# Attention scores over 128 rows: the queries' low part padded with zeros

## The chip, the cores and the metric

The kernel runs on one core of one Trainium2 chip, in one launch. The metric is the device time of a run in microseconds (us). Of the kernel before there are three timed runs and one profiled execution.

## What is computed

The reference is a block of two layers over 256 tokens (`x`) and 256 context tokens (`ctx`), 1024 features wide, in float32. Layer 0 mixes by neighbourhood attention with 16 heads of 64 features, layer 1 by a gated linear recurrence; each is followed by a feed-forward part, and every step is modulated by vectors worked out from a condition. The change lies in the attention of layer 0:

```python
q, k, v = jnp.split(h @ w_qkv, 3, axis=-1)
q = rms_norm(q.reshape(B, n, NA_HEADS, NA_HEAD_DIM), q_gain) * scale
k = rms_norm(k.reshape(B, n, NA_HEADS, NA_HEAD_DIM), k_gain)
...
s_loc = jnp.einsum('bqhd,bjqwhd->bhqjw', q_row, k_win) + bias.transpose(0, 2, 1, 3)[None]
s_ctx = jnp.einsum('bqhd,bkhd->bhqk', q_row, k_c)
s = jnp.concatenate([s_loc.reshape(B, NA_HEADS, GRID_W, n_loc), s_ctx], axis=-1)
p = jax.nn.softmax(s.astype(jnp.float32), axis=-1).astype(v_win.dtype)
```

The grid has 4 rows of 64 columns. A latent token sees 16 columns of each of the 4 rows and the whole context; a context token sees the context.

## The kernel before

Products run in a rounded form of float32 (`F32R`). To keep the precision, each operand is split in a high part (the rounded value) and a low part (what is left), and a product is hi*hi + hi*lo + lo*hi. `prod` (L404 to L415) does this for all weights; its matmul is L410, the line that fills most of TensorE's time. `split` (L402, L403) makes the two parts of the weights, the high one on ScalarE, the low one on VectorE.

`setup` (L68 to L190) loads the inputs and does the first products of the attention's queries, keys and values while the modulation vectors are still being worked out (`ada_first`, L266). Its buffers lie in a pool that is closed at its end; the pool of the attention takes the same memory.

`na` (L451) goes over 4 groups of 4 heads. For each it makes queries, keys and values from weight blocks of 256 columns (L410, through `toks`), normalises queries and keys (L475 to L480), and calls `na_pair` for two pairs of heads. `ada` (L298 for the loads, L216 for the products) works out further modulation vectors on the side, from blocks `ada_raw` with two buffers. The output projection follows (L410 with `oh`, `ol`).

`na_pair` (L519) does one pair of heads:

- GpSimd builds the table `tb` of biases and masks: it clears a part (L523), loads four pieces through its own DMA queue (L531), changes the sign (L534) and masks (L537, L541). Two buffers take turns.
- TensorE transposes queries and keys (L550), so that a head's 64 features lie in 64 partitions, the first head's in the lower half, the second head's in the upper.
- Per head (`a` = 0, 1), a key tile `ks` holds the high part in the head's own half and the low part in the other half (L561, L562). A query tile `qs` holds the high part in both halves (L566). The queries' low part goes to the head's own half of one tile `ql` that both heads share (L567).
- `scores` (L574) makes the logits with two products: L577 over 128 rows gives q_hi * k_hi + q_hi * k_lo; L578 over the 64 rows of the head's own half adds q_lo * k_hi. Per pair, four calls have 512 columns of keys (two tiles of latent queries for each head), and four have 256 (the context's). That makes 64 of L577 and 64 of L578 in the kernel.
- The softmax: VectorE adds the bias and takes the minimum (L599, the signs being changed) or takes the minimum alone (L631), ScalarE takes the exponential (L582), VectorE scales (L583, L584), TensorE transposes (L611, L635), and the products with the values follow (L649, L657), then the split of the output (L663, L664).

The two heads of a pair run as two generators in turn. A scheduler of the framework orders the instructions of each engine before the run: it places products of the next group's weights (L410) between the steps of the softmax. Each engine works through its own list in order.

```python
nc.tensor.matmul(ps, qs[a][:, t], ks[a][:, kr], start=True, stop=False, skip_group_check=True)
nc.tensor.matmul(ps, ql[f, t], ks[a][f, kr], start=False, stop=True, skip_group_check=True)
```

Of the kernel before, what the change touches and what calls it, by code (L numbers as in the profile page):

```python
# [8 lines left out]
F32 = mybir.dt.float32  # L9
# [22 lines left out]
# which modulation vectors are worked out when  # L32
# [4 lines left out]
def cap(ap, off, dims):  # L37
    """A free pattern of one's own over the partitions of ap."""
    return bass.AP(ap.tensor, ap.offset + off, [list(ap.ap[0])] + [list(d) for d in dims])


class Block:
# [19 lines left out]
    def mixed(self):  # L62
        """Banks of the three tags in turn, where nothing else asks for them."""
        self.turn = (getattr(self, "turn", -1) + 1) % 7
        return self.bank(("mm", "ax0", "ax1", "mm", "ax0", "ax1", "mm")[self.turn])

# [1 line left out]
    def setup(self):  # L68
# [16 lines left out]
        with ExitStack() as ctx:  # L85
# [56 lines left out]
            for k in range(KT):  # L142
                if k == 4:
                    # the factors of the first norm, in all partitions
# [13 lines left out]
            # the first products start on the features whose modulation is there already; one accumulation  # L158
            # group per bank
# [48 lines left out]
    def ada_rows(self, tiles, cs=None):  # L208
        """The products of silu(c), silu(c_ctx) with 4 blocks of 256 columns, as columns over the features."""
# [21 lines left out]
    def ada_put(self, l, m, k0, nj, cols, j0):  # L231
        """cols: the features of nj blocks from block j0 on, to be those from k0 on of vector m."""
# [20 lines left out]
    def ada_first(self, ip, qd):  # L253
        """Shift and scale of layer 0's first norm, for a quarter of the features."""
# [36 lines left out]
    def ada(self, l, params, pool=None):  # L291
        """Modulation vectors of layer l, as columns over the features, for both streams."""
        nc = self.nc
        for m in params:
            def tiles():
                for k in range(KT):
                    w = (pool or self.apool).tile([P, D], F32, name="ada_raw", tag="ada_raw")
                    nc.sync.dma_start(w, self.in_ada_w[l, k * P : (k + 1) * P, m * D : (m + 1) * D])  # L298
                    yield w

            self.ada_put(l, m, 0, 4, self.ada_rows(tiles()), 0)

    def ada_aside(self, params, pool, eng=None):
        """The same, step by step: the sums over blocks of 128 by the vector engine, those within by TensorE."""
        nc = self.nc
        eng = eng or nc.vector
        for l, m in params:
            # what follows layer 1's mixing is asked for the latents alone
# [20 lines left out]
    def norm_add(self, k, r):  # L329
        nc = self.nc  # L330
        if k == 0:
            nc.scalar.square(self.acc[:, r], self.x[k][:, r])
            if r.start == 0:
                # has the table of the function in place by the time that norm_end asks for it
# [37 lines left out]
    def weights_in_ctx(self, ap):  # L372
        """The same, in the context's half of h, which nothing else needs any more."""
# [10 lines left out]
    def weights(self, ap, pieces=4, pool=None):  # L384
        """A block of weights [nk*128, 256] as its two parts."""
# [19 lines left out]
    def prod(self, out, pairs, start=True, stop=True):  # L405
        """out += sum over the pairs of (hi, lo) of both sides."""
# [12 lines left out]
    def feat(self, out, w, m, r):  # L419
        """out [128 features of the block's half m, tokens r]"""  # L420
# [4 lines left out]
    def toks(self, out, w, tt, ks=range(KT), start=True, stop=True):  # L425
        """out [128 tokens of tile tt, the block's 256 features]"""
# [4 lines left out]
    def rsqrt(self, u):  # L431
        """u ** -0.5 of a few columns."""
# [18 lines left out]
    def na(self):  # L451
# [4 lines left out]
        ol = [np_.tile([P, T], F32R, name=f"ol{k}", bufs=1) for k in range(KT)]  # L456
        wq = self.in_na_w_qkv[0]
# [61 lines left out]
    def na_pair(self, np_, pr, j, qn, v, oh, ol):  # L519
# [5 lines left out]
        for u in range(2):  # L525
            # partition 64 u + i: row 1 - u of the tile's two, column 63 - i; with the sign changed, as the
            # logits' (their minimum is then the bias that the exponential asks for)
# [17 lines left out]
        # per head: queries [hi; hi] and keys [hi; lo], one above the other (its own half first), and  # L545
        # the queries' low parts; the queries of each tile go from the last to the first
# [7 lines left out]
        ql = np_.tile([P, T], F32R, name="ql", tag="ql", bufs=1)  # L554
        qs, ks = [], []
        for a in range(2):
# [8 lines left out]
            for half in (own, other):  # L565
                nc.scalar.activation(cap(qa[half], P - 1, back), src, AF.Copy, scale=self.q_gain[own])  # L566
            nc.vector.scalar_tensor_tensor(  # L567
                cap(ql[own], P - 1, back), src, self.q_gain[own], cap(qa.bitcast(F32)[own], P - 1, back),
# [5 lines left out]
        def scores(ps, a, q, kr):  # L574
            f = slice(64 * a, 64 * a + 64)
            t = slice(q * P, (q + 1) * P)
            nc.tensor.matmul(ps, qs[a][:, t], ks[a][:, kr], start=True, stop=False, skip_group_check=True)  # L577
            nc.tensor.matmul(ps, ql[f, t], ks[a][f, kr], start=False, stop=True, skip_group_check=True)  # L578
# [166 lines left out]
    def hgrn(self):  # L745
# [66 lines left out]
        for mc in range(4):  # L812
# [13 lines left out]
            if mc < 3:  # L826
                # one accumulation group for the bank: the heads come one after the other
# [14 lines left out]
    def hgrn_head(self, gp, h, m, sg, v, q):  # L842
        nc = self.nc
        # slots of xq: q forward, k forward, k backward, q backward
# [14 lines left out]
        # states after the context, one per direction  # L859
# [31 lines left out]
        # the products q k, by levels of blocks of 1, 2, 4, ... tokens: those within 32 tokens  # L891
        # lie in dc, the others in am
# [27 lines left out]
        for lg in range(7):  # L920
# [30 lines left out]
            for dr in range(2):  # L951
                # forward: q of odd blocks and k of even ones; backward: k of odd and q of even
# [16 lines left out]
        # through the whole of what comes before: the states' share  # L969
# [16 lines left out]
        else:  # L986
            # no other table is asked for until the norm that follows
# [11 lines left out]
    def finish(self, ctx):  # L999
# [4 lines left out]
        def after(mt, s, c):  # L1004
# [7 lines left out]
            # the last ones go out each on its own  # L1012
# [66 lines left out]
```

## Time and profile before

| | |
|---|---|
| time, three runs | 1185.1, 1185.15, 1188.06 us (median 1185.15) |
| profiled execution: its span | 1180.4 us; its own time is not listed apart, and the fastest run lies 4.7 us above it |
| busy share of the span | PE 98%, PEld 84%, DVE 67%, ACT 43%, POOL 6% |
| mean granted TensorE clock | 0.997 |
| HBM read | 166.82 MB, 142 GB/s over the span |

The profile names the engines PE (TensorE's products), PEld (its weight loads), DVE (VectorE), ACT (ScalarE), POOL (GpSimd) and SP (SyncE, here a DMA queue). The span is the time from the first to the last instruction of one execution. Products are pipelined on PE: a row's duration overlaps the next row's, and its end is modelled, so the distance between the starts of two rows tells how fast they follow each other.

### The profile page before, as it was taken

How to read it: one execution, taken by the hardware profiler on the slowest of the kernel's cores; microseconds unless marked ns; L12 is line 12 of the kernel's file. 1: busy time of each engine (PE TensorE's matmuls, PEld its weight loads, DVE VectorE, ACT ScalarE, POOL GpSimd, SP SyncE). 2: the span in 40 equal slices, each digit the busy share in tenths (PEclk: the TensorE clock that was granted, in tenths of full speed). 3: DMA queues.
4: the chain of work that ended last, by engine and by line, in shares of the span. 5: the costliest groups of instructions: out<-in, count | busy, mean ns of one | idle time of the engine just before them, and what ended most of it. 6: DMA issues, size and time to landing. Idle time of an engine off the chain costs nothing.

```text
span 1180.4 us, 21338 instructions
## 1 busy us (share of the span) xinstructions
PE 1155.7 (98%) x8539; PEld 989.7 (84%) x8539; DVE 786.3 (67%) x1872; ACT 502.1 (43%) x1079; POOL 76.5 (6%) x119
## 2 busy tenths in 40 slices
PE   6989999999999999999999999999999999999998
PEld 5967779786798788778888789979797989999998
DVE  4588676866679583845373668686868687665543
ACT  5346553736544322221332344434344355555442
POOL 1224232320000000000000000000000000000000
PEclk9989999999999999999999999999999999999999
DMA  9863372235116462646372552212232336655662
GB/s 330 267 184 88 86 167 73 51 85 179 56 52 217 142 228 74 194 146 221 105 234 91 173 176 71 96 63 95 72 108 73 108 113 237 219 177 185 201 211 89
DMA packets 134402, 169.23 MB, mean 143 GB/s; under 512 B 4608, under 2 KB 122272, under 8 KB 134304
## 3 DMA queue, kind: packets, MB, share of 16 engines
q1 hardware_dynamic: 132368, 164.64, 42.1%
q0 software_dynamic: 1728, 3.17, 3.1%
q8 instruction: 67, 1.10, 0.4%
q14 instruction: 31, 0.25, 0.1%
q10 hardware_dynamic: 208, 0.07, 0.0%
HBM read 166.82 MB, written 1.05 MB: 142 GB/s over the span
## 4 chain that ended last, share of the span: by engine, by line
PE 91%; DVE 5%; DMA 3%; ACT 1%; issue 0%; ACTq 0%; SPq 0%
PE mm L410 50%; PE ax L410 27%; PE ax L578 2%; PE ada_ps L216 2%; PE ax L577 2%; DMA ada_raw<-in_ada_w_dram 1%; PE ax L611 1%; PE ax L649 1%; DVE w_lo L403 1%; PE ax L900 1%; PE ax L883 1%; PE ada_ps L266 1%; DMA xt<-in_ctx_dram 1%; PE ax L946 1%; PE ax L635 1%; PE ax L550 0%
## 5 line engine op out<-in xcount | busy, mean ns | idle before, releaser
L403 DVE TENSOR_TENSOR w_lo<-w_raw,w_hi 128x512 fp32r<-128x512 f32 (+1 forms) x448 | 273.7, 647 | 129.1 <-ACT w_hi L402 126.7
L402 ACT CAST w_hi<-w_raw 128x512 fp32r<-128x512 f32 (+1 forms) x448 | 237.8, 583 | 229.4 <-PE mm L410 100.4
L410 PE MATMUL mm<-hl,w_hi 128*128 128x256 f32 (+1 forms) x608 | 201.3, 332 | 0.0
L410 PE MATMUL mm<-hh,w_lo 128*128 128x256 f32 (+1 forms) x608 | 200.6, 330 | 0.0
L410 PE MATMUL mm<-hh,w_hi 128*128 128x256 f32 (+1 forms) x608 | 198.4, 328 | 0.0
L410 PE MATMUL ax<-hh,w_lo 128*128 128x256 f32 (+1 forms) x400 | 131.1, 328 | 0.2 <-DVE w_lo L403 0.2
L410 PE MATMUL ax<-hh,w_hi 128*128 128x256 f32 (+1 forms) x400 | 131.0, 328 | 0.0
L410 PE MATMUL ax<-hl,w_hi 128*128 128x256 f32 (+1 forms) x400 | 130.9, 327 | 0.0
L410 PE MATMUL mm<-w_hi,hh 128*128 128x256 f32 x448 | 128.0, 286 | 0.8 <-ACT hh L366 0.8
L410 PE MATMUL mm<-w_hi,hl 128*128 128x256 f32 x448 | 127.4, 284 | 0.0
L410 PE MATMUL mm<-w_lo,hh 128*128 128x256 f32 x448 | 127.2, 284 | 0.0
L410 PEld LDWEIGHTS mm<-hl,w_hi 128*128 128x128 f32 x608 | 114.1, 188 | 11.3
L410 PEld LDWEIGHTS mm<-hh,w_lo 128*128 128x128 f32 x608 | 114.1, 188 | 10.9
L410 PEld LDWEIGHTS mm<-hh,w_hi 128*128 128x128 f32 x608 | 113.8, 188 | 11.2 <-ACT hh L366 0.8
L319 DVE SCALAR_TENSOR_TENSOR ada_acc<-ada_raw,cs,ada_acc 128x1024 f32<-128x1024 f32 x63 | 79.0, 1280 | 18.7 <-DMA ada_raw<-in_ada_w_dram 18.5
L410 PEld LDWEIGHTS mm<-w_hi,hh 128*128 128x128 f32 x448 | 85.6, 191 | 6.4 <-issue 4.7
L410 PEld LDWEIGHTS mm<-w_hi,hl 128*128 128x128 f32 x448 | 85.1, 190 | 3.6 <-issue 3.1
L410 PEld LDWEIGHTS mm<-w_lo,hh 128*128 128x128 f32 x448 | 85.0, 190 | 2.9 <-issue 2.7
L410 PEld LDWEIGHTS ax<-hh,w_hi 128*128 128x128 f32 x400 | 75.1, 188 | 7.9 <-ACT w_hi L402 0.8
L410 PEld LDWEIGHTS ax<-hh,w_lo 128*128 128x128 f32 x400 | 75.0, 188 | 7.5 <-DVE w_lo L403 0.4
L410 PEld LDWEIGHTS ax<-hl,w_hi 128*128 128x128 f32 x400 | 75.1, 188 | 7.3
L694 ACT CAST mid_h<-sa 128x512 fp32r<-128x512 f32 (+1 forms) x44 | 22.5, 512 | 91.8 <-DVE sa L691 91.8
(277 smaller groups left out, 2150.4 us busy)
## 6 DMA issues: line engine op xcount, KB each, us to landing
w_raw<-in_ffn_w_in_dram SPq DMA_DIRECT2D x44, 1024.0 KB, 5.0
ada_raw<-in_ada_w_dram SPq DMA_DIRECT2D x80, 512.0 KB, 4.5
w_raw<-in_hg_w_in_dram SPq DMA_DIRECT2D x20, 1024.0 KB, 4.8
w_raw<-in_na_w_qkv_dram SPq DMA_DIRECT2D x9, 1024.0 KB, 5.0
ada_first<-in_ada_w_dram SPq DMA_DIRECT2D x32, 256.0 KB, 5.8
w_raw<-in_ffn_w_out_dram SPq DMA_DIRECT2D x8, 896.0 KB, 4.6
w_raw<-in_ffn_w_out_dram SPq DMA_DIRECT2D x8, 768.0 KB, 4.3
w_raw<-in_ffn_w_out_dram SPq DMA_DIRECT2D x8, 640.0 KB, 4.2
```

The source lines that it names most:

```text
L216: nc.tensor.matmul(ps[32 * j : 32 * j + 32, 0:256], cs[:, k, :], w[:, j * 256 : (j + 1) * 256], start=(k == 0), stop=(k == last), tile_pos ...
L266: nc.tensor.matmul(ps[32 * j : 32 * j + 32, 0:P], self.cs[:, k, :], w[:, j // 2, (j % 2) * P : (j % 2 + 1) * P], start=(k == 0), stop=(k = ...
L319: eng.scalar_tensor_tensor(acc[s], w, c, acc[s], op0=ALU.mult, op1=ALU.add)
L402: self.nc.scalar.copy(wh[:, ks], raw[:, ks])
L403: self.nc.vector.tensor_tensor(wl[:, ks], raw[:, ks], wh.bitcast(F32)[:, ks], op=ALU.subtract)
L410: self.nc.tensor.matmul(out, a, b, start=(start and i == 0 and j == 0), stop=(stop and i == n - 1 and j == 2), skip_group_check=True,)
L577: nc.tensor.matmul(ps, qs[a][:, t], ks[a][:, kr], start=True, stop=False, skip_group_check=True)
L578: nc.tensor.matmul(ps, ql[f, t], ks[a][f, kr], start=False, stop=True, skip_group_check=True)
L611: nc.tensor.transpose(tp[:, kt * P : (kt + 1) * P], sb[:, kt * P : (kt + 1) * P], self.ident)
L635: nc.tensor.transpose(tp[:, kt * 256 + i * P : kt * 256 + (i + 1) * P], sb[:, i, kt * P : (kt + 1) * P], self.ident)
L649: nc.tensor.matmul(o[64 * a : 64 * a + 64, 0:256], v[:, kt, j * P + 64 * a : j * P + 64 * a + 64], pts[a][0][:, kt], start=(kt == 0), stop ...
L694: nc.scalar.copy(mh, sa)
```

## The change

The tile `ql` becomes two tiles, one per head, made once at the start of the attention. GpSimd writes zeros into the other head's half of each. The low part is written to the head's own half as before. The second score product takes all 128 rows of the query tile and of the key tile; the rows with zeros add nothing to the sum. `ql0` takes the slot in which the norm's sum `acc` is kept later, `ql1` lies in the attention's pool. The changed file has also lost its comments and gained two lines, so that lines of `na_pair` carry other numbers (L577 and L578 are L579 and L580, L523 and L531 are L527 and L535).

```diff
     def na(self):
...
         ol = [np_.tile([P, T], F32R, name=f"ol{k}", bufs=1) for k in range(KT)]
+
+        self.ql = [self.spool.tile([P, T], F32R, name="ql0", tag="acc", bufs=1), np_.tile([P, T], F32R, name="ql1", bufs=1)]
+        for a in range(2):
+            nc.gpsimd.memset(self.ql[a][64 - 64 * a : 128 - 64 * a].bitcast(F32), 0.0)
         wq = self.in_na_w_qkv[0]
...
         back = [[P, 4], [-1, P]]
-        ql = np_.tile([P, T], F32R, name="ql", tag="ql", bufs=1)
         qs, ks = [], []
...
             nc.vector.scalar_tensor_tensor(
-                cap(ql[own], P - 1, back), src, self.q_gain[own], cap(qa.bitcast(F32)[own], P - 1, back),
+                cap(self.ql[a][own], P - 1, back), src, self.q_gain[own], cap(qa.bitcast(F32)[own], P - 1, back),
                 op0=ALU.mult, op1=ALU.subtract,
             )
...
         def scores(ps, a, q, kr):
-            f = slice(64 * a, 64 * a + 64)
             t = slice(q * P, (q + 1) * P)
             nc.tensor.matmul(ps, qs[a][:, t], ks[a][:, kr], start=True, stop=False, skip_group_check=True)
-            nc.tensor.matmul(ps, ql[f, t], ks[a][f, kr], start=False, stop=True, skip_group_check=True)
+            nc.tensor.matmul(ps, self.ql[a][:, t], ks[a][:, kr], start=False, stop=True, skip_group_check=True)
```

On GpSimd's list (POOL) the two clearings come in ahead of work that was there. Before, from the last small clearing of `setup` to the loads of the second pair's table; names in brackets are the counters that an instruction waits for (of DMA queues, of engines):

```order
L83 MEMSET pick 128x1
L99 DMA rows<-in_hg_lower_dram 32x128 [waits Pool_49]
L100 DMA rows<-in_hg_norm_g_dram 1x16x8
...
L103 DMA rows<-in_na_k_gain_dram 1x16x4 x2
L523 MEMSET tb 128x256 [waits DMAHW6_49,DMAHW7_49,DMAHW0_49,PE_49]
L531 DMA tb<-in_na_rpb_dram 64x6x64 x2
L531 DMA tb<-in_na_rpb_dram 64x6x64 [waits DMASW0_49]
L531 DMA tb<-in_na_rpb_dram 64x6x64 [waits DMASW1_49]
L523 MEMSET tb 128x256 [waits DMAHW2_49,DMAHW1_49,PE_49]
```

The same stretch of the changed kernel:

```order
L83 MEMSET pick 128x1
L460 MEMSET ql_879 64x512 [waits Pool_49]
L99 DMA rows<-in_hg_lower_dram 32x128
L100 DMA rows<-in_hg_norm_g_dram 1x16x8
...
L103 DMA rows<-in_na_k_gain_dram 1x16x4 x2
L460 MEMSET ql_880 64x512 [waits DVE_49,PE_49]
L527 MEMSET tb 128x256 [waits DMAHW1_49,DMAHW7_49,DMAHW0_49,Pool_49]
L535 DMA tb<-in_na_rpb_dram 64x6x64 x2
L535 DMA tb<-in_na_rpb_dram 64x6x64 [waits DMASW0_49]
L535 DMA tb<-in_na_rpb_dram 64x6x64 [waits DMASW1_49]
L527 MEMSET tb 128x256 [waits DMAHW3_49,DMAHW2_49]
```

One clearing (`ql_879`, the first head's tile) now stands ahead of the small loads for `rows`. The other (`ql_880`) waits for VectorE and TensorE and stands ahead of both tables `tb`, whose own wait for TensorE is gone in exchange.

TensorE's list (PE) keeps its order around the scores. In the first pair's context scores it was:

```order
L577 MATMUL ax_1068<-ks_987,qs_986 128x256
L578 MATMUL ax_1068<-ks_987,ql 128x256
L577 MATMUL ax_1089<-ks_994,qs_993 128x256
L578 MATMUL ax_1089<-ks_994,ql 128x256
L577 MATMUL ax_1089<-ks_994,qs_993 128x256
L578 MATMUL ax_1089<-ks_994,ql 128x256
```

and is in the changed kernel, at the same place:

```order
L579 MATMUL ax_1071<-ks_990,qs_989 128x256
L580 MATMUL ax_1071<-ks_990,ql_879 128x256
L579 MATMUL ax_1092<-ks_997,qs_996 128x256
L580 MATMUL ax_1092<-ks_997,ql_880 128x256
L579 MATMUL ax_1092<-ks_997,qs_996 128x256
L580 MATMUL ax_1092<-ks_997,ql_880 128x256
```

Only the tile with the low part is another; the one move on this list lies in `setup`, where a transposition of `rows` (L119) comes behind three more transpositions of the input. SP's list is the same.

## Rows read from the trace of the kernel before

**Rows 1.** The page: TensorE's share, the chain by engine, one line of weight loads.

```profile
PE 1155.7 (98%) x8539; PEld 989.7 (84%) x8539; DVE 786.3 (67%) x1872; ACT 502.1 (43%) x1079; POOL 76.5 (6%) x119
...
PE 91%; DVE 5%; DMA 3%; ACT 1%; issue 0%; ACTq 0%; SPq 0%
...
L410 PEld LDWEIGHTS mm<-hl,w_hi 128*128 128x128 f32 x608 | 114.1, 188 | 11.3
```

**Rows 2.** Busy us by stretch: from:to, length, PE, PEld, DVE, ACT, POOL, clock, DMA.

```profile
83.00:310.00 227.00, 224.37 (x1585) 171.91 (x1578) 165.32 (x453) 123.15 (x267) 53.67 (x60) 1.00 0.39 99
```

**Rows 3.** Line L578: its products, and who waited for them (us, times).

```profile
L578 PE MATMUL ax<-ks,ql x64: 379/383/502, 84.2 to 301.3; 64*128 64x512 f32 x32, 64*128 64x256 f32 x32
...
  DVE sm_mc L631: 5.2, 15
  DVE sb L599: 3.1, 8
```

**Rows 4.** Timeline, PE: start, duration, line; the eighth pair's context scores.

```profile
300.32 0.39 PE L577 MATMUL ax<-ks,qs 128*128 128x256 f32 x1
300.63 0.38 PE L578 MATMUL ax<-ks,ql 64*128 64x256 f32 x1
```

**Rows 5.** Timeline, PE: products of 128 rows, of 256 and of 512 columns.

```profile
120.46 0.29 PE L410 MATMUL mm<-w_lo,hh 128*128 128x256 f32 x1
120.58 0.28 PE L410 MATMUL mm<-w_hi,hl 128*128 128x256 f32 x1
...
302.14 0.39 PE L410 MATMUL mm<-oh,w_hi 128*128 128x512 f32 x1
302.37 0.39 PE L410 MATMUL mm<-ol,w_hi 128*128 128x512 f32 x1
```

**Rows 6.** Timeline, PE: a single L578 within work of 128 rows.

```profile
83.86 0.40 PE L577 MATMUL ax<-ks,qs 128*128 128x512 f32 x1
84.19 0.49 PE L578 MATMUL ax<-ks,ql 64*128 64x512 f32 x1
84.61 0.38 PE L410 MATMUL mm<-w_hi,hl 128*128 128x256 f32 x1
84.83 0.28 PE L410 MATMUL mm<-w_hi,hh 128*128 128x256 f32 x1
```

**Rows 7.** Timeline, first and third pair: a scaling on VectorE, the transposes that read it.

```profile
91.93 0.49 DVE L584 TENSOR_SCALAR sb<-sb,sm_l 128x512 f32<-128x512 f32 x1
...
92.57 0.63 PE L611 MATMUL ax<-ident,sb 128*128 128x128 f32 x4
...
154.03 0.34 DVE L584 TENSOR_SCALAR sbc<-sbc,sm_l 128x256 f32<-128x256 f32 x1
...
155.49 0.38 PE L635 MATMUL ax<-ident,sbc 128*128 128x128 f32 x2
```

**Rows 8.** Timeline, POOL: the first two pairs' tables.

```profile
45.96 0.31 POOL L523 MEMSET tb<- 128x256 f32 x1 [40.61 <-PE ada_ps L266]
...
61.28 0.66 POOL L531 DMA_DIRECT2D tb<-in_na_rpb_dram  x1
67.94 2.16 POOL L534 TENSOR_SCALAR tb<-tb 128x768 f32<-128x768 f32 x1 [6.00 <-DMA tb<-in_na_rpb_dram]
```

**Rows 9.** Timeline, PE: the last first product; the wait for ada_raw.

```profile
62.84 0.28 PE L410 MATMUL ax<-w_hi,hl 128*128 128x256 f32 x1
...
71.73 1.08 PE L216 MATMUL ada_ps<-ada_raw,cs 128*32 128x256 f32 x8 [4.58 <-DMA ada_raw<-in_ada_w_dram]
```

**Rows 10.** Timeline, VectorE: first read of the table; a small operation twice.

```profile
82.72 0.17 DVE L441 SCALAR_TENSOR_TENSOR rq_y<-rq_b,rq_y 128x8 f32<-128x8 f32 x1
...
85.87 0.69 DVE L599 CUSTOM_DVE_ANT_1 sb<-ax,tb 128x512 f32<-128x512 f32 x1
...
102.69 0.69 DVE L441 SCALAR_TENSOR_TENSOR rq_y<-rq_b,rq_y 128x8 f32<-128x8 f32 x1
```

**Rows 11.** DMA queues, 40 to 110 us: packets, MB, share of 16 engines.

```profile
q0 software_dynamic: 576, 1.18, 17.8%
```

## The prediction

> **What bounds the kernel now.** I read the page first, then the busy time by stretch, then the two score lines, then the timeline of TensorE around them. The page shows a TensorE-bound kernel: PE is busy 98% of the span and carries 91% of the chain that ended last [rows 1]. The change touches one stage, the neighbourhood attention from about 83 to 310 us, and there too PE is busy 224.37 of 227 us, VectorE 165.32, ScalarE 123.15 [rows 2]. So what TensorE saves there shortens the run, unless a chain of softmax steps on VectorE or ScalarE ends later than TensorE's filler work. Those chains are short of slack at places, and this is the main uncertainty.
>
> The second score product (L578) runs 64 times over 64 rows, with a median of 383 ns [rows 3], but durations on PE are modelled; what counts is the distance from one start to the next. Where L577 and L578 alternate at 256 columns, they stand 0.31 us apart [rows 4]. Products of 128 rows behind products of 128 rows stand 0.12 us apart at 256 columns and 0.23 us at 512 [rows 5]. So the alternation costs 0.195 us at each change of the row count.
>
> A single L578 inside 128-row work pays for the way there and the way back, spread over three rows: 83.86 to 84.19 (0.33 for 0.23), 84.19 to 84.61 (0.42 for 0.23), 84.61 to 84.83 (0.22 for 0.12) [rows 6]. That is 0.97 for 0.58: **0.39 us per excursion** to 64 rows, the number that the alternation gives too (2 x 0.195). A product of 64 rows is not slower in itself: late is each product that comes behind one of another row count, and the next one's successor a little.
>
> **The change part by part.**
>
> *The second product over 128 rows.* Nothing is added: 64 loads and 64 products with the same columns. The excursions go. In the order of TensorE's rows nine of the 64 stand directly behind another L578, which leaves 55 excursions. Of these, 49 lead back to 128x128 work: 49 x 0.39 = 19.1 us. Four lead into the modulation products of L216, which use another shape of their own; there one of the two changes stays, so 4 x 0.2 = 0.8. In the last two, three L578 stand in a row; they pay little now, and I take nothing. Freed on TensorE: **about 20 us**.
>
> *How much of it reaches the end.* Per pair of heads some 1.2 us are freed in the first four score products and 1.3 in the last four. Behind each lies a chain: minimum on VectorE, exponential on ScalarE, scaling on VectorE, then transposes on PE, which fills the time with products of L410. The filler stays as long as it is, so TensorE would arrive at the transposes earlier by what was freed, and gets it only as far as the chain also moves or has spare time. The chain moves where VectorE waits for L578 now: 3.1 us in the first halves and 5.2 in the second [rows 3]. The spare time is from the end of a scaling to the start of its transposes. Tight is the first pair, 91.93 + 0.49 = 92.42 to 92.57, or 0.15 us; wide is the third pair's second half, 154.03 + 0.34 = 154.37 to 155.49, or 1.12 [rows 7]. Read so for each pair and half, and the least of each taken, the spare time is 4.7 us over eight first halves and 5.5 over eight second ones; about 0.1 of each of the 16 is signalling that cannot be used, which leaves 8.6. Together 8.6 + 8.3 = **16.9 us** get through; 3 are lost to waits of the transposes. If the spare time were worth nothing, 8.3 would be left; if the chains moved fully, 20. I take 16.9, the ends go into the range.
>
> *A new wait on POOL.* The two tiles are cleared by GpSimd at the start of the stage. The first lies in memory of its own and only stands ahead of the small loads for `rows`; their transposition stands on TensorE's list behind that of nearly all of the input, so it costs nothing; if that cover were gone, it would be one clearing, twice the columns of the 0.31 us in [rows 8], some 0.5 us. The second lies where the third weight block of the first products was, and the built program has it wait for the last TensorE product that reads that block: L410 at 62.84 [rows 9]. On POOL's queue both tables of biases (`tb`) of the first two pairs stand behind it. They begin at 45.96 now [rows 8], and would begin at about 63.5. Building the first takes 45.96 to 61.28, 15.3 us, so it would be there at 79; its first reader is VectorE's L599 at 85.87 [rows 10]. Seven us of cover: by itself the delay costs nothing.
>
> What it costs is company. TensorE stands still from 67 to 71.73 for a block of `ada_raw` [rows 9], the one long DMA wait of the stage. Until now only the last `tb` load (issued 61.28, waited for until 67.94 [rows 8]) is in its way; after the change five more are issued between 64 and 72. Twelve such loads took 17.8% of 16 engines over 70 us [rows 11], or 1.04 us of all engines each, so the wait grows by 0 (they come behind the block) to 5.2 us (all five ahead of it). I take **+2**: the weights and the block are issued before or along with the first `tb` load, so less than half should be ahead.
>
> *POOL beside VectorE.* While POOL builds `tb`, small VectorE operations are held: L441 on 128x8 took 0.69 us at 102.69 beside a POOL operation, and 0.17 at 82.72 without one [rows 10], 0.52 more. The second pair's table is worked on from 67.94 [rows 8], and 17.5 us later from about 85.5, beside the first pair's softmax: up to four such delays, 2.1 us; nothing if they fall into waits. I take **+1.5**, nearer the upper end because VectorE is dense there.
>
> *Where the tiles lie.* The first shares its slot with the norm's sum, which is written only after all heads' outputs are projected, behind the last L578. VectorE's writes (L567) keep their shape. Nothing.
>
> Sum: -16.9 + 2 + 1.5 = **-13.4 us**. The span of the profiled execution would go from 1180.4 to 1167.0. The median of the runs shown stands 4.75 us above that span; I move it by the same amount: 1185.15 - 13.4 = **1171.8 us**.
>
> **The rivals.**
>
> *All of it arrives.* The chains move with TensorE, and the `tb` loads slip behind the block. For it: PE has hardly a wait on VectorE in the stage. Against it: the 0.15 us of the first pair [rows 7]. -20: 1165.
>
> *VectorE takes over.* Only what VectorE waits for now is gained, and POOL's delays cost their 3.5: -8.3 + 3.5 = -4.8: 1180.4.
>
> *Loads of 128 rows show.* Each new weight load is paid in full: 64 x 0.188 = 12.0 of the 20 come back, 8 are freed, 6.8 get through at the same share; with the 3.5 the time is 1185.15 - 3.3 = 1181.9. Against it: products of 256 columns stand 0.12 us apart [rows 5] while each load takes 0.188 [rows 1], so loads of 128 rows do run beside products. The Trainium skill, "TensorE: Matmul & The Clock Gate", section "Part 3: Packing small matmuls — row/col tiling", says that a weight load overlaps products in flight only where the row groups differ, which speaks against this change. By that rule the time is this rival's; the trace of L410 does not agree with it.
>
> *The price is not the row count's.* If the 0.2 us came from the change of operands, it would stay, and POOL's 3.5 would come on top: 1188.7. Against it: L410 changes operands at each product and stands 0.12 apart [rows 5].
>
> *The table comes too late: slower.* The place is L599 of the first pair. It decides from the point where `tb` takes over 22 us to build rather than 15.3. If the six loads on POOL's queue took turns at the 6.7 us of the one issued at 61.28 [rows 8], they alone would take 40 us, 24.7 more than the whole build now; less 7 of cover that is +17.7, and -13.4 + 17.7 = +4.3: 1189.5. Against it: 6.7 is mostly the way of a single load, and the first four, issued one behind the other, are in within the 15.3 us now.
>
> **How the numbers follow.** My forecast has 0.53, "all of it arrives" 0.20, "VectorE takes over" 0.17, "loads show" 0.05, "table too late" 0.03, "not the row count" 0.02. A measurement tells 0.3% (3.6 us) from no change: below 1181.6 counts as faster, above 1188.7 as slower. Forecast and first rival are faster; of VectorE's rival, which ends near the border, 0.12: faster 0.85. Its other 0.05 and the shown loads make 0.10 for the same; the last two rivals 0.05 for slower. The range reaches from the first rival, 1164, to just past VectorE's, 1181; what lies outside is the shown loads, the slower cases and a part of VectorE's, under 2 in 10.
>
> **What would show it right or wrong.** Right: the second product's rows over 128 rows, 0.12 and 0.23 us behind the first; POOL's second clearing at about 63 us, `tb` behind it; the wait for `ada_raw` ending near 74 rather than 71.73; from there to the end of the attention some 15 us less; waits of the transposes on VectorE's scaling a few us longer. Wrong: starts still 0.31 us apart, a first L599 that waits for POOL, or a stage from 83 us on that is shorter by under 8 us.

## The result and the profile after

The changed kernel took a median of 1167.89 us (four runs, 1166.43 to 1171.54), the kernel before beside it 1185.45 (1185.1 to 1188.06). The ratio is 0.9859 with a 95% interval of 0.9837 to 0.9880, or -16.7 us (-19.3 to -14.2); a second comparison gave 0.9849 (0.983 to 0.9869). The forecast was 1171.8, in a range of 1164 to 1181.

The page of the changed kernel: busy time by engine, the granted clock over 40 slices, the chain of waits by engine and by line. To be compared with [rows 1].

```profile
PE 1138.9 (98%) x8539; PEld 987.2 (85%) x8539; DVE 778.7 (67%) x1872; ACT 501.7 (43%) x1079; POOL 74.5 (6%) x121
...
PEclk9999999999999999999999999999999999999999
...
PE 90%; DVE 4%; DMA 3%; ACT 2%; issue 1%; ACTq 0%; DVEq 0%
```

PE has lost 16.8 us of busy time with the same number of products, and is still the bound. The span went from 1180.4 to 1166.3. The last pair's context scores, the counterpart of [rows 4], in PE's timeline (start, duration, engine, line):

```profile
283.85 0.28 PE L580 MATMUL ax<-ks,ql 128*128 128x256 f32 x1
283.96 0.28 PE L579 MATMUL ax<-ks,qs 128*128 128x256 f32 x1
284.08 0.28 PE L580 MATMUL ax<-ks,ql 128*128 128x256 f32 x1
...
284.43 0.39 PE L410 MATMUL mm<-ol,w_hi 128*128 128x512 f32 x1
```

From start to start 0.12 us have passed instead of 0.31. A single second product among L410, the counterpart of [rows 6]:

```profile
81.58 0.40 PE L579 MATMUL ax<-ks,qs 128*128 128x512 f32 x1
81.81 0.40 PE L580 MATMUL ax<-ks,ql 128*128 128x512 f32 x1
82.05 0.28 PE L410 MATMUL mm<-w_hi,hl 128*128 128x256 f32 x1
82.16 0.28 PE L410 MATMUL mm<-w_hi,hh 128*128 128x256 f32 x1
```

The distances are 0.23, 0.24 and 0.11: nothing of the excursion is left. Added up over all 64 second products and the two rows behind each, the starts stood 20.8 us above the distances of [rows 5] before and 1.7 after: **19.1 us freed**, where 20 were forecast.

How much arrives, by stretches from one pair's first score product to that of the next, the last stretch the fifth to eighth pair together (columns as in [rows 2]). Before:

```profile
83.86:108.74 24.88, 23.76 (x158) 16.37 (x157) 21.22 (x56) 14.82 (x33) 9.60 (x10) 1.00 0.51 132
108.74:140.65 31.91, 31.91 (x242) 26.16 (x243) 21.83 (x64) 16.43 (x36) 9.64 (x10) 1.00 0.27 49
140.65:164.03 23.38, 22.76 (x173) 15.30 (x173) 19.09 (x52) 15.38 (x34) 7.95 (x10) 1.00 0.76 206
164.03:205.65 41.62, 41.57 (x321) 36.34 (x320) 27.89 (x83) 18.30 (x40) 9.54 (x11) 1.00 0.33 81
205.65:301.26 95.61, 94.77 (x635) 71.27 (x636) 71.38 (x191) 53.78 (x117) 16.93 (x20) 1.00 0.38 97
```

And after:

```profile
81.58:104.44 22.86, 21.77 (x158) 15.88 (x157) 19.68 (x55) 14.69 (x33) 12.81 (x15) 1.00 0.66 157
104.44:134.60 30.16, 30.10 (x243) 25.85 (x243) 21.93 (x64) 16.22 (x36) 10.09 (x12) 1.00 0.28 50
134.60:159.17 24.57, 21.30 (x173) 15.00 (x173) 19.31 (x53) 16.44 (x35) 7.90 (x10) 1.00 0.73 196
159.17:198.33 39.16, 39.10 (x321) 35.85 (x320) 27.80 (x82) 16.94 (x38) 9.51 (x11) 1.00 0.35 85
198.33:284.32 85.99, 85.54 (x636) 69.47 (x637) 67.29 (x190) 53.52 (x116) 16.57 (x20) 1.00 0.41 108
```

The attention is 217.40 - 202.74 = **14.7 us** shorter (14.2 in the second profile of the changed kernel). In the last four pairs all arrives: 95.61 to 85.99, or 9.6, and 9.6 of the 19.1 were freed there. In the first four 9.6 were freed too, and 5.0 arrive. The third pair's stretch is 1.2 us *longer* than before, though PE is busy 1.5 less in it. What stands still there shows in PE's timeline:

```profile
156.46 0.64 PE L216 MATMUL ada_ps<-ada_raw,cs 128*32 128x256 f32 x8 [2.57 <-DMA ada_raw<-in_ada_w_dram]
157.69 0.64 PE L216 MATMUL ada_ps<-ada_raw,cs 128*32 128x256 f32 x8 [0.59 <-DMA ada_raw<-in_ada_w_dram]
```

At the same place before:

```profile
161.30 0.64 PE L216 MATMUL ada_ps<-ada_raw,cs 128*32 128x256 f32 x8
162.56 0.64 PE L216 MATMUL ada_ps<-ada_raw,cs 128*32 128x256 f32 x8 [0.62 <-DMA ada_raw<-in_ada_w_dram]
```

A wait of 0.6 us has become two of 3.2 in all. The queue that brings the block (SP) shows why. Before, a block of `w_raw` was issued, and behind it four blocks of `ada_raw`, merged in one row that starts with the first:

```profile
149.90 0.38 SPq L395 DMA_DIRECT2D w_raw<-in_na_w_qkv_dram  x1
154.02 9.57 SPq L298 DMA_DIRECT2D ada_raw<-in_ada_w_dram  x4
```

And after:

```profile
143.68 0.38 SPq L395 DMA_DIRECT2D w_raw<-in_na_w_qkv_dram  x1
146.61 12.10 SPq L298 DMA_DIRECT2D ada_raw<-in_ada_w_dram  x4
```

TensorE comes to the first of these `ada_raw` blocks 7.4 us earlier than before (153.89 for 161.30), and the block is issued 7.4 us earlier too, but it lands only 4.8 us earlier: at 156.42 for 161.26, which was 0.04 us ahead of its use. The `w_raw` block goes out only 6.2 us earlier, so `ada_raw` now follows it by 2.9 us instead of 4.1 and takes 9.8 us from its issue instead of 7.2. In seven profiles (these two, the second of the changed kernel and four runs below) that time is 7.2 to 7.5 us where the block follows by 4.0 to 4.4, 8.1 at 3.3, and 9.7 to 10.2 at 2.9 to 3.0. What TensorE waited for between the first and last score product (us in total, times, longest) is, before,

```profile
PE ax L577 <- DVE ks L562: 1.1, 1, 1.1
PE ada_ps L216 <- DMA ada_raw<-in_ada_w_dram: 0.6, 1, 0.6
PE ax L635 <- DVE sm_l L583: 0.5, 1, 0.5
...
```

and after,

```profile
PE ada_ps L216 <- DMA ada_raw<-in_ada_w_dram: 4.0, 3, 2.6
PE ax L579 <- ACT qs L569: 0.3, 1, 0.3
```

POOL, to be set against [rows 8]:

```profile
62.88 0.52 POOL L460 MEMSET ql<- 64x512 f32 x1 [57.23 <-PE ax L410]
63.34 0.30 POOL L527 MEMSET tb<- 128x256 f32 x1
...
75.36 2.14 POOL L538 TENSOR_SCALAR tb<-tb 128x768 f32<-128x768 f32 x1 [7.56 <-DMA tb<-in_na_rpb_dram]
...
79.85 1.54 POOL L545 TENSOR_SCALAR_AFFINE_SELECT tb<-tb 64x576 f32<-64x576 f32 x2
```

The clearing and the tables moved as forecast, but the first table is ready at 79.85 + 1.54 = 81.4, not at 79. Its first reader on VectorE did not have to wait for it:

```profile
83.53 0.69 DVE L601 CUSTOM_DVE_ANT_1 sb<-ax,tb 128x512 f32<-128x512 f32 x1
```

Of the seven us of cover 2.1 were left (5.0 in the second profile of the changed kernel).

### The profile page after: what moved, and what is told of

It is laid out like the page before. It is cut to its first block, busy times and chain, and to the rows that moved or that the text cites. A ratio compares the mean times of both kernels' runs of the same rounds, so it can differ in the third digit from the quotient of the medians.

```text
span 1166.3 us, 21342 instructions
## 1 busy us (share of the span) xinstructions
PE 1138.9 (98%) x8539; PEld 987.2 (85%) x8539; DVE 778.7 (67%) x1872; ACT 501.7 (43%) x1079; POOL 74.5 (6%) x121
## 4 chain that ended last, share of the span: by engine, by line
PE 90%; DVE 4%; DMA 3%; ACT 2%; issue 1%; ACTq 0%; DVEq 0%
PE mm L410 49%; PE ax L410 28%; DMA ada_raw<-in_ada_w_dram 3%; PE ada_ps L216 2%; PE ax L651 2%; PE ax L902 1%; PE ax L613 1%; PE ax L579 1%; PE ax L637 1%; PE ax L885 1%; PE ax L580 1%; PE ada_ps L266 1%; ACT qs L569 1%; DVE w_lo L403 1%; PE ax L948 1%; PE ax L659 1%
## 5 line engine op out<-in xcount | busy, mean ns | idle before, releaser
L410 PE MATMUL mm<-hl,w_hi 128*128 128x256 f32 (+1 forms) x608 | 201.6, 333 | 0.0
L410 PE MATMUL mm<-hh,w_lo 128*128 128x256 f32 (+1 forms) x608 | 201.3, 332 | 0.0
L410 PE MATMUL mm<-hh,w_hi 128*128 128x256 f32 (+1 forms) x608 | 199.1, 329 | 0.0
L410 PE MATMUL ax<-hh,w_lo 128*128 128x256 f32 (+1 forms) x400 | 131.7, 330 | 0.0
L410 PE MATMUL ax<-hh,w_hi 128*128 128x256 f32 (+1 forms) x400 | 131.7, 329 | 0.0
L410 PE MATMUL ax<-hl,w_hi 128*128 128x256 f32 (+1 forms) x400 | 131.3, 328 | 0.0
L410 PE MATMUL mm<-w_hi,hh 128*128 128x256 f32 x448 | 126.3, 282 | 0.8 <-ACT hh L366 0.8
L410 PE MATMUL mm<-w_lo,hh 128*128 128x256 f32 x448 | 125.7, 280 | 0.0
L410 PE MATMUL mm<-w_hi,hl 128*128 128x256 f32 x448 | 125.5, 280 | 0.0
L410 PEld LDWEIGHTS mm<-hl,w_hi 128*128 128x128 f32 x608 | 114.1, 188 | 11.4
L410 PEld LDWEIGHTS mm<-hh,w_lo 128*128 128x128 f32 x608 | 114.0, 188 | 11.3
L410 PEld LDWEIGHTS mm<-hh,w_hi 128*128 128x128 f32 x608 | 113.8, 188 | 10.9 <-ACT hh L366 0.8
L410 PEld LDWEIGHTS mm<-w_hi,hh 128*128 128x128 f32 x448 | 84.6, 189 | 5.1 <-issue 3.2
L410 PEld LDWEIGHTS mm<-w_hi,hl 128*128 128x128 f32 x448 | 84.2, 188 | 2.0 <-issue 1.6
L410 PEld LDWEIGHTS mm<-w_lo,hh 128*128 128x128 f32 x448 | 84.2, 188 | 1.8 <-issue 1.4
L410 PEld LDWEIGHTS ax<-hh,w_hi 128*128 128x128 f32 x400 | 75.2, 188 | 7.6 <-ACT w_hi L402 0.8
L410 PEld LDWEIGHTS ax<-hl,w_hi 128*128 128x128 f32 x400 | 75.1, 188 | 7.4
L410 PEld LDWEIGHTS ax<-hh,w_lo 128*128 128x128 f32 x400 | 74.9, 187 | 7.4 <-DVE w_lo L403 0.2
```

The costliest lines, as they stand in the source:

```text
L410: self.nc.tensor.matmul(out, a, b, start=(start and i == 0 and j == 0), stop=(stop and i == n - 1 and j == 2), skip_group_check=True,)
```

## The experiments

Theory A, the forecast's: the row count cost 0.39 us per excursion, and what doesn't arrive is lost to the softmax chains. Theory B: what doesn't arrive is lost in waits for `ada_raw`, since TensorE now reaches blocks that its DMA queue hasn't brought yet. The late clearing on POOL is a third question.

**The changed kernel once more**, beside the next three runs.

> The changed kernel once more beside the others: 1166 to 1169 us, and the first score product at 81.6 us if that is no chance.

Measured: 1168.75 us (five runs), the kernel before 1186.95 (17 runs), ratio 0.9849. The first score product came at 84.37, not at 81.6, so the earlier start in the first profile is not the change's doing.

**The late clearing taken away.** `ql1` gets memory that nobody waits for; the tables are built at 40 us as before.

```diff
+        ql1 = np_.tile([P, T], F32R, name="ql1", bufs=1)
...
-        self.ql = [self.spool.tile([P, T], F32R, name="ql0", tag="acc", bufs=1), np_.tile([P, T], F32R, name="ql1", bufs=1)]
+        self.ql = [self.spool.tile([P, T], F32R, name="ql0", tag="acc", bufs=1), ql1]
```

> The changed kernel, with the second head's tile at the front of the attention's pool, over memory that is free early, so that its clearing waits for nothing late and the bias tables begin at about 46 us again; the second product keeps its 128 rows. Theory A (POOL's move gained some 2.3 us, because POOL no longer holds VectorE's splits at 54 to 62 us and the weight and modulation loads go out sooner): first score product back at about 83.9 us, the wait for ada_raw back at about 4.6 us with the half clock behind it, 1170 us. Rival B (the earlier start of the scores in the profile of the changed kernel was chance, POOL's move is worth nothing or costs): first score product where it was in the changed kernel or earlier, 1166 to 1168 us.

Measured: 1173.3 us (six runs, 1167.99 to 1175.9), ratio 0.9879 (0.9857 to 0.9901). The first score product came at 83.77, as theory A said, behind one wait for `ada_raw` of 5.7 us, where it said 4.6; but the time lies above both theories. No gain from early tables shows. This kernel is 4.5 us *above* the changed one of the same series, though the intervals of the two overlap. Its granted clock was 0.50 from 158.8 to 165.6 us and from 70.0 to 76.8; how much of the 4.5 that makes is not shown.

**The late clearing alone.** The tiles, zeros and waits of the change, but the second product over the head's own 64 rows.

```diff
-            nc.tensor.matmul(ps, self.ql[a][:, t], ks[a][:, kr], start=False, stop=True, skip_group_check=True)
+            f = slice(64 * a, 64 * a + 64)
+            nc.tensor.matmul(ps, self.ql[a][f, t], ks[a][f, kr], start=False, stop=True, skip_group_check=True)
```

> The changed kernel with the second product over the 64 rows of the head's own half again; the two tiles and the late clearing stay. Theory A: first score product at about 81.6 us, starts of alternating score products 0.31 us apart, the attention as long as before (217 us from the first to the last score product), 1183 us. Rival B: nothing gained before the scores, 1185 to 1187 us.

Measured: 1187.31 us (12 runs), ratio 1.0004 (0.9992 to 1.0017), or +0.5 us with bounds of -0.9 and +2.0. The attention took 217.91 us, 217.40 in the kernel before. So clearing, late tables and POOL beside VectorE cost nothing that shows, and **the padding carries the whole gain**. The 0.31 us are there as before:

```profile
302.20 0.39 PE L579 MATMUL ax<-ks,qs 128*128 128x256 f32 x1
302.52 0.38 PE L581 MATMUL ax<-ks,ql 64*128 64x256 f32 x1
```

**Fewer changes of the row count, the same 64-row products.** In the kernel before, the context's scores in the order full, full, low, low. (With this order the context's logits are not the reference's; number and sizes of the score products are the same.)

```diff
...
-            for i in range(2):
-                scores(ps[:, i * 256 : (i + 1) * 256], a, 2 + i, CTX)
+            for part in range(2):
+                for i in range(2):
+                    scores(ps[:, i * 256 : (i + 1) * 256], a, 2 + i, CTX, part)
```

> The kernel before, with the context's four products of a head in the order full, full, low, low instead of full, low, full, low: as many 64-row products, but 16 excursions to 64 rows fewer. Theory A (the price is per change of the row count, 0.39 us per excursion): 16 x 0.39 = 6.2 us freed, about 5 get through, 1180 us. Rival (the price belongs to each 64-row product): no change, 1185 us.

Measured: 1182.33 us, ratio 0.9956 (0.9939 to 0.9973), -5.2 us; the excess around the second products fell by 6.5, the attention by 5.8. In PE's rows 40 excursions are left of 55, 15 fewer rather than 16. The last pair's context scores, two rows merged in each line:

```profile
295.56 0.48 PE L578 MATMUL ax<-ks,qs 128*128 128x256 f32 x2
295.97 0.50 PE L580 MATMUL ax<-ks,ql 64*128 64x256 f32 x2
296.40 0.50 PE L578 MATMUL ax<-ks,qs 128*128 128x256 f32 x2
```

Four products now take 0.84 us, 4 x 0.31 = 1.24 before. No 64-row product is gone, only about half of the context's changes. So the price is that of the change, not of the 64 rows.

**Half the dose.** The changed kernel, padded rows for the latent queries' products (512 columns) alone.

```diff
-            nc.tensor.matmul(ps, self.ql[a][:, t], ks[a][:, kr], start=False, stop=True, skip_group_check=True)
+            f = slice(0, P) if kr != CTX else slice(64 * a, 64 * a + 64)
+            nc.tensor.matmul(ps, self.ql[a][f, t], ks[a][f, kr], start=False, stop=True, skip_group_check=True)
```

> The changed kernel with the padded rows used by the 512-column products of the latent queries alone; the context's second products, of 256 columns, run over the head's own 64 rows again. The tiles, their clearing and the order of the work are those of the change. Theory 1 (0.39 us per excursion, whatever the columns; the latent products have about half of the 55): about 9 to 10 us of the 19.4 stay freed, the time lies near 1177, 8 us above the changed kernel. Theory 2 (the price grows with the columns, as a second product of 512 columns is twice as long): two thirds of the gain stay, near 1173. Theory 3 (the first halves' chains, which had the least spare time, absorb what is freed there): near 1183 or above.

Measured: 1178.06 us, ratio 0.9939 (0.9918 to 0.9960). 7.2 us stay freed, not the 9 to 10 that I wrote. The latent products have 23 of the 55 excursions, because nine already stood behind one another; that makes 9.0 at 0.39 each, and four of the 23 lead into products of L216, two of these from three L578 in a row, for which the prediction took less or nothing. A price in proportion to columns, with two thirds of the gain, is out. From first to last score product it took 211.79 us, 5.6 less than before:

```profile
83.69:295.48 211.79, 209.45 (x1526) 166.19 (x1525) 158.94 (x439) 117.45 (x255) 57.59 (x65) 1.00 0.43 105
```

**Shorter softmax chains.** The changed kernel without reciprocal and scaling.

```diff
-            nc.vector.reciprocal(l, l)
-            nc.vector.tensor_scalar_mul(p, p, l)
```

> The changed kernel without the reciprocal and the scaling of the softmax: the probabilities are left unnormalised, so the attention's values are not the reference's. This takes some 26 us of VectorE's work and one step out of each chain between score product and transposes. Theory 1 (of the 19.4 us freed, some 2 to 3 are lost because the transposes wait for the softmax chain): 2 to 3 us come back, first to last score product goes from 202.7 to about 200. Theory 2 (the chains cost nothing, all that is lost is the wait for ada_raw at the third pair's start): within 1 us of the changed kernel. Theory 3 (VectorE has become the bound of the stage): a gain much above 3 us.

Measured: 1172.5 us, ratio 0.9893 (0.9872 to 0.9914), above the changed kernel, though the interval overlaps that of the first comparison. The attention took 201.88 us, 0.9 less: theory 2 by that length. VectorE's work in the attention fell from 156.0 to 125.5 us and next to nothing came of it. What TensorE waited longest for there:

```profile
PE ada_ps L216 <- DMA ada_raw<-in_ada_w_dram: 5.3, 1, 5.3
```

With shorter chains the wait for the block grew, from 4.0 us at three places to 5.3 at one: what TensorE doesn't spend on the softmax it spends there, which is theory B's direction. The scheduler placed other work in the freed room, so the two kernels differ in order too, and twice a stretch of 6.8 us ran at clock 0.50, one of them within the attention.

**The block's place.** Two runs move a modulation vector to the third group of heads, which had none: from the first group (`NA_ADA = ((), (4,), (2,), (3,))`), and from the second.

```diff
-NA_ADA = ((2,), (4,), (), (3,))
+NA_ADA = ((2,), (), (4,), (3,))
```

> The changed kernel, with the modulation vector of the second group of heads moved to the third, which had none. Theory 1 (the new wait for ada_raw at 153.6 to 157.7 us, 3.8 us of gaps against 1.0 before, is where part of the freed time goes): the gap goes, first to last score product falls from 202.7 to 199 to 200.5, and the time by 2 to 4 us to about 1164 to 1166. Theory 2 (the wait only takes the place of one on the softmax chain or on w_raw): the gap goes, the length from first to last score product stays within 1 us. Theory 3 (the third group's start has the same traffic, table loads and weight blocks): the same gap appears one group later, time the same.

Measured: 1169.82 us, ratio 0.9865 (0.9843 to 0.9887), no gain. The stretches of the third and of the fifth pair:

```profile
136.28:156.34 20.06, 19.70 (x148) 16.77 (x149) 17.79 (x51) 14.60 (x33) 8.30 (x10) 1.00 0.41 74
...
191.81:216.49 24.68, 21.70 (x173) 15.47 (x173) 19.70 (x53) 16.41 (x35) 7.40 (x9) 0.98 0.74 199
```

In the third pair 24.57 us have become 20.06, and the fifth, 20.01 in the changed kernel, took 24.68, with waits of 2.9 for `ada_raw`. The attention took 203.13 us, 0.4 more. The wait goes where the vector goes: theory 3.

> The changed kernel, with the modulation vector that is worked out beside the first group of heads moved to the third group, which had none. Theory 1 (the waits for ada_raw at 66 to 81 us are time lost to the DMA): the gaps there, 5.9 us in the changed kernel's profile, go, the third group has other weights to hide the blocks behind, and the time falls by 4 to 6 us, to 1162 to 1164; the first score product starts near 75 to 77 us instead of 81.58. Theory 2 (the DMA queue is full there whatever is asked of it): the w_raw blocks of the first group's own weights are awaited instead, the time stays within 2 us of the changed kernel's. Theory 3: the third group, whose softmax has the most spare time, pays the same wait later: first score product earlier by 4 to 6 us, the attention's length longer by as much, time the same.

Measured: 1166.55 us (four runs, 1162.85 to 1166.96), ratio 0.9829 (0.9806 to 0.9853). The first score product came at 78.82; the attention itself took 204.56 us, 1.8 more than in the changed kernel. (Of the 5.9 us in the expectation 0.8 belong to a wait at 87 us; ahead of the first score product it was 5.1.) So 2.8 us were gained ahead of the scores, less than theory 1 asks, and 1.8 of them given back within, as theory 3 has it. It is the fastest complete version, but its interval overlaps the changed kernel's, so it isn't shown to beat it.

**The blocks left away, in both kernels.** One block of `ada_raw` per vector instead of eight, the products kept.

```diff
-                    w = (pool or self.apool).tile([P, D], F32, name="ada_raw", tag="ada_raw")
-                    nc.sync.dma_start(w, self.in_ada_w[l, k * P : (k + 1) * P, m * D : (m + 1) * D])
+                    w = w if l == 0 and k else (pool or self.apool).tile([P, D], F32, name="ada_raw", tag="ada_raw")
+                    l == 0 and k or nc.sync.dma_start(w, self.in_ada_w[l, k * P : (k + 1) * P, m * D : (m + 1) * D])
```

> The changed kernel, with one block of ada_raw loaded for each modulation vector of the attention instead of eight: all eight products of a vector read that block, so these three vectors (and what they scale) are not the reference's. The products stay, 21 transfers of 512 KB and their waits go. Theory 1 (of the 19.1 us freed in the attention some 4 are given back in waits for ada_raw, all in the first four pairs, and hardly any in the softmax): first to last score product falls from 202.7 to between 198 and 199.5. Theory 2 (the softmax chains take up what TensorE no longer waits for): it stays above 201.5. Either way the waits at 66 to 81 us go, so the first score product starts at 75 to 78 us; the time is 1155 to 1162 by theory 1, above 1162 by theory 2.

> The kernel before with the same edit: one block of ada_raw for each modulation vector of the attention, so the same vectors are not the reference's. TensorE's order is that of the changed kernel with the same edit. Theory 1 (the waits for ada_raw appear in the attention because TensorE is faster, not because the blocks come later): first to last score product falls by only 0.6 to 1, to about 216.5, and the padding is worth 18 to 19 us between these two kernels, against 14.7 with all loads in place. Theory 2 (the softmax chains limit what gets through): the two differ by 14 to 15 us, as the kernels with all loads do.

Measured: 1159.42 us (ratio 0.9765, 0.9747 to 0.9784) and 1181.5 (0.9944, 0.9929 to 0.9959). The first four and the last four pairs, with the changed kernel's scores:

```profile
77.38:190.30 112.92, 110.55 (x876) 92.96 (x876) 87.43 (x258) 64.35 (x140) 42.76 (x50) 1.00 0.37 68
190.30:276.35 86.05, 85.65 (x632) 69.58 (x633) 67.06 (x190) 53.57 (x116) 16.59 (x20) 1.00 0.29 65
```

And with those of before:

```profile
82.85:202.70 119.85, 118.17 (x877) 94.51 (x877) 89.17 (x258) 64.79 (x140) 35.97 (x40) 1.00 0.31 63
202.70:298.14 95.44, 94.67 (x632) 71.04 (x632) 71.12 (x191) 53.80 (x117) 16.96 (x20) 1.00 0.26 59
```

The attention's 198.97 us with the changed scores lie in theory 1's window, and the first score product came at 77.38. But the two differ by 16.3 us in the attention, between the 14 to 15 of theory 2 and the 18 to 19 of theory 1. (The times differ by 22.1. In the two profiles 5.5 of that lie ahead of the scores, where the kernel with the old ones ran at clock 0.50 from 72.7 to 76.1, and 4.8 behind the attention, of which the last section tells.) In the first four pairs 6.9 of 9.6 freed us arrive, where 5.0 did with all loads. The other 2.7 are in small waits for the softmax; the longest with the changed scores:

```profile
PE ax L613 <- DVE sm_l L585: 0.9, 2, 0.6
PE ax L613 <- DVE sb L586: 0.8, 3, 0.3
```

These waits are longer than they look, since a row's modelled end covers the start of the next wait. PE's rows come in the same order with both scores, so the distance from each row's start to the next can be set against its counterpart, and the differences added up. In the first four pairs that gives, with all loads, 9.6 us less for the second products and the rows behind them, 0.5 less for the other first products, 3.4 more for the products that read `ada_raw` and 1.5 more for the transposes of the probabilities. With the blocks left away it gives 9.6 less, nothing more for `ada_raw` and 2.8 more for the transposes.

So both theories hold in part. Of the 4.5 us lost in the first four pairs, 1.9 come back when the blocks are no longer awaited, although 3.4 more were spent waiting for them: most of the rest becomes a wait for VectorE.

## Why the prediction was right, and where it wasn't

*The price of the row count.* Right: 19.1 us freed against 20. That the grouped order, with 15 excursions fewer and all 64-row products left, gave 5.2 us shows that the distance of starts was the right reading. The duration of a row would have misled: its median is 383 ns before [rows 3] and 376 after. The rival of 1188.7 is out as well: the operands change at each product as before, and the 0.2 us are gone. The Trainium skill, "TensorEngine Tiling (Array Packing)", section "Key Properties", states that a change of the tiling mode drains TensorE, with no time for it; the runs agree that a change costs time, 0.195 us, but do not show that a drain is the cause.

*Nothing is paid for loads of 128 rows.* Right, and the rival of 1181.9 is out. The loads that the change made larger take 188 ns each, and the products between them stand 0.12 us apart:

```profile
L580 PEld LDWEIGHTS ax<-ks,ql x64: 186/188/193, 81.6 to 284.2; 128*128 128x128 f32 x64
```

The Trainium skill, "TensorE: Matmul & The Clock Gate", section "Part 3: Packing small matmuls — row/col tiling", has in its list of what overlaps that a load does so only where row groups differ; here load and product both use all rows, and the trace doesn't agree with it.

*16.9 of 20 get through, 3 are lost to transposes that wait for the scaling.* This is the step that failed, in its size and in most of its reason. 14.7 got through, and all that was lost, some 4.5, was lost in the first four pairs: 3.4 to the wait for `ada_raw`, which the step left out, and 1.5 to the transposes, where it had 3 (the first products give 0.5 back). There the spare time was used up as forecast: the second pair's first scaling ends at 110.79, its transposes start at 110.85. With the blocks left away the transposes lose 2.8, so the mechanism was real, and the other wait came ahead of it. In the last four pairs the transposes stand 0.7 us closer than before: the chains moved along entirely, and the rival "all of it arrives" was right. Nowhere was "VectorE takes over". What I missed: the freed time moves TensorE and the issue of the `ada_raw` block alike, by 7.4 us, but not the transfers that the block shares its way with. It now follows the `w_raw` block more closely, on DMA engines that are busy for 0.73 of that stretch, and takes 2.6 us longer; before, it landed 0.04 us ahead of its use. I had priced that wait only at 67 us, where POOL's move would lengthen it, and not at 154, where nothing but the gain itself does.

*+2 for the longer wait at 67 us, +1.5 for POOL beside VectorE.* Both too large: together 3.5 was forecast, and the run with the late clearing alone measured +0.5 (-0.9 to +2.0). The wait was split more than lengthened: from one of 4.6 us to three of 5.1 in all (two of 5.3 in the second profile). The first block is there earlier, at 68.39 instead of 71.73, and later ones are awaited in its place; that the tables' loads hold them up fits the run with early tables, which has one wait again, but is not shown apart. VectorE's small operations (L439 to L441 on 128x8) were held, to over 0.4 us, 11 times between 80 and 300 us, 12 times before, and never without a POOL operation beside them: they were as many as before, so nothing came on top. The first score product came at 81.58 and 84.37 in the two profiles of the changed kernel, at 83.86 before.

*The table's cover.* Its delay costs nothing, as I said, but with less to spare: the build took 18.0 us rather than 15.3, and with the scores 2.3 us earlier the first reader came at 83.53 rather than 85.87. Of the seven us 2.1 were left, and in the second profile 5.0; the last rival did not come near.

*The sum.* That it came so near is in part luck: 16.9 for 14.7 is 2.2 too much gain, 3.5 for about 0.5 is 3.0 too much cost, and the two nearly cancel. The attention's 14.7 less nothing elsewhere would give 1170.5 from the 1185.15 of the forecast, and 1167.9 was measured. Whether the remaining 2.6 are a gain is not settled: 14.7 lies within the first comparison's interval (14.2 to 19.3) and just outside the second's (15.5 to 20.2). In the profiles shown 2.3 lie ahead of the first score product: the kernel before ran at half clock from 70.9 to 77.7, and its L410 rows in that stretch stand 2.1 us further apart in all than the changed kernel's, whose first profile has no such stretch. Its second profile has one of 3.4 us and starts the scores at 84.37, so these 2.3 are not the padding's.

## What to carry to other kernels

Where products of fewer rows stand among products of all rows, look at the distance of starts behind each of them, and pad with zeros (or group them) if it stands above that of equal rows: 0.2 us per change were to be had here for two clearings. Ask of each microsecond freed on the bounding engine what it then meets earlier: here a block that landed 0.04 us ahead of its use was awaited for 2.6 us afterwards. Of the gain a part went into such waits, and moving that load only moved the wait. Taking it away brought back 1.9 of the 3.4 us, since the softmax was next in line.

## What was not expected of the hardware

The same products in the last feed-forward part follow each other at two distances, and which one is not the kernel's doing. PE over the same 25 us, without a wait, in the two profiles of the changed kernel (1166.3 us span, then 1165.6):

```profile
1015.00:1040.00 25.00, 25.00 (x214) 25.00 (x214) 13.44 (x25) 12.05 (x27) 0.00 (x0) 1.00 0.57 188
```

```profile
1015.00:1040.00 25.00, 25.00 (x223) 25.00 (x222) 13.87 (x26) 11.88 (x25) 0.00 (x0) 1.00 0.64 213
```

214 products against 223 at the same granted clock, 25 / 214 = 0.117 us against 0.112; the profile of before had 223. From 1000 to 1100 us that is worth 3.7 us, more than 0.3% of the run, so part of the difference of two profiles' spans is this alone. Of the twelve profiles four show the shorter distance (the kernel before, the second of the changed kernel, the vector moved from the first group, one block with the changed scores), the others the longer one.

The granted clock fell to half (from 2.4 to 1.2 GHz) behind waits of TensorE, and not behind all. Before, TensorE stood still from 67.15 to 71.73, and the clock was 0.50 from 70.9 to 77.7 us:

```profile
70.90:77.70 6.80, 5.97 (x33) 4.12 (x34) 4.84 (x24) 0.00 (x0) 2.29 (x4) 0.50 0.84 284
```

With the wait split into pieces of at most 2.1 us, the first profile of the changed kernel has no such stretch ahead of its end, not even behind its wait of 2.57 at 156 us. Its second profile has two of 3.4 us, one from 74.1, at the end of a wait of 4.1, the other from 159.4, behind a wait of 2.96.
